# Layer 2 of a two-layer block kernel: attention by pairs of heads, with the products of two heads in turns in the two halves of the TensorE array

## The chip, the core and the metric

The kernel runs on one core of a Trainium2 chip. A core has a matrix engine (TensorE; PE in the profile), and VectorE (DVE), ScalarE (ACT), GpSimd (POOL) and SyncE (SP), each with an instruction queue of its own. Matmuls read SBUF and write PSUM; DMA queues bring the weights from device memory. The metric is the device time of one execution in microseconds; 0.2% of this kernel is 3.1 us.

## What is computed

The reference is two transformer blocks on a sequence of 256 tokens with a width of 1024. The first has a stick-breaking attention, a retention branch and a mixture of 32 experts; the change does not touch it. The second, cut to what matters:

```
h = rms_norm(x, norm1_pre)
q, k, v, z, xbc, dt_raw, gates = split(h @ w_in)      # 8 query heads and 2 key heads of 64; z, xbc: state space branch
attn_out = softmax(q k^T / 8) v                       # per head: 256 x 256 scores; then @ w_attn_proj
xs, bm, cm = split(silu(conv(xbc)))                   # 16 heads of 64, 2 groups, state 128
y = ssd_forward + ssd_backward + d_skip * xs          # per head: (C B^T * decay) X, and a term from the state
ssd_y = rms_norm(y * silu(z))                         # then @ w_ssd_proj
x += rms_norm((g_attn * attn_out + g_ssd * ssd_out) @ w_out)
x += rms_norm((silu(gate) * up) @ w_down)             # feed forward, width 2816
```

Two head loops matter here. Attention: for each of 8 heads the scores (256 x 256, from q and k of depth 64), a softmax, and the product with v (64 columns). State space: for each of 16 heads a 256 x 256 block-wise decay matrix, and its product with that head's 64 columns of `xs`.

## The kernel before

`mixer2` (layer 2 up to the first residual) runs two kinds of work woven into each other. The backbone is a row of large projections (`lin_t`, lines 241 to 243, tiles `pt_lin`; `lin`, lines 214 to 216): each weight chunk is brought by DMA into a ring (`raw`), split by ACT and DVE into a high and a low part (`whi`, line 168, and `wlo`, line 169, a ring of three), and multiplied in three matmuls. Between these steps stand small pieces: `decay`, `values`, `scores`, `probs`, `attend`, convolutions, norms. Table `STEPS2` gives each piece a place among the steps, `weave` calls it there, and a scheduler then fixes the order on every engine when the program is built, so what stands next to what on PE is not what the code's order alone says.

The pieces which the change touches:

- `decay(h)`, 16 heads: two matmuls make a log decay matrix `pr` (lines 1532 and 1533), ACT takes four exponentials into `E` (line 1538), DVE multiplies (line 1539), POOL adds the two directions (line 1541). Every second head adds a matmul `peb` (line 1546).
- `values(c)`, 8 pairs of heads: line 1560 multiplies `E` with 64 columns of `xs` into one half of the PSUM tile `py`: partitions 0 to 63 for the even head, 64 to 127 for the odd one. First both products of the even head, then both of the odd one. Line 1562 adds the state's product with the whole array. DVE then makes `y`.
- `scores(h)`, 8 heads: line 1577, two matmuls with a depth of 64 (the even head's q and k are in partitions 0 to 63, the odd head's in 64 to 127) into a PSUM tile `psc`; DVE takes the row maximum `mx` (lines 1579, 1580); ACT takes two exponentials with their sums (line 1585), DVE the reciprocal, ACT scales (line 1588): `prob`.
- `probs(h)`: four transposes (line 1596, tile `ptp`) and a copy `pT` by ACT (line 1598).
- `attend(h)`: line 1608, two matmuls with 64 columns of v into one half of the PSUM tile `pov`; after the odd head ACT and DVE split the result for the projection.
- `attn(i)`, ten steps: `scores(i)`, `probs(i - 1)`, `attend(i - 2)`.

A matmul that uses only half of the array's rows is shown as `64*128` in the profile, one that uses half of its columns as `128*64`, and one that uses the whole as `128*128`. Every fp32 matmul other than a transpose leaves two records (passes): 16 score matmuls are 32 records. The projections' matmuls leave one. The PSUM pool `pm` (tag `m`) has four buffers, shared by `psc`, `ptp`, `pov`, `pr`, `peb` and some others; SBUF tag `E` has four, shared by `E`, `prob` and `pT`.

Of the kernel before, what the change touches and what calls it, by code (L numbers as in the profile page):

```python
# [10 lines left out]
F32 = mybir.dt.float32  # L11
F32R = mybir.dt.float32r
I32 = mybir.dt.int32
AF = mybir.ActivationFunctionType
ALU = mybir.AluOpType
AX = mybir.AxisListType
PSUM = bass.MemoryType.PSUM
P = 128
D = 1024
T = 256  # L20
# [29 lines left out]
def blk(b):  # L50
    return slice(b * P, b * P + P)
# [40 lines left out]
class Net:  # L92
# [1154 lines left out]
    def mixer2(self):  # L1247
        nc, a, tc, xt = self.nc, self.a, self.tc, self.xt
        with ExitStack() as es:
            p1 = self.pool(es, "m2a")  # L1250
            p2 = self.pool(es, "m2b", 2)
            pw = self.pool(es, "pslinD", 3, space=PSUM)
            py_ = self.pool(es, "psyD", 1, space=PSUM)
            pm = self.pool(es, "psmD", 4, space=PSUM)
            w = a["w_in_2"][0]
            ident, ones = self.ident, self.ones
            K = {}
# [8 lines left out]
            def after(name):  # L1266
                return tc.issue_after(K[name].ins)

            def exps():
                return after("silu")  # L1270
# [56 lines left out]
            xs = p1.tile([P, 2, D], F32, name="xs")  # L1327
# [52 lines left out]
            bias = p1.tile([P, 2, 2, 16], F32, name="bias")  # L1380
# [74 lines left out]
            qT = p1.tile([P, 4, T], F32, name="qT", tag="qT")  # L1455
            kT = p1.tile([P, 2, T], F32, name="kT")
            vt = p1.tile([P, 2, P], F32, name="vt")
            Q = {}
# [51 lines left out]
            E, EB, ST = {}, {}, {}  # L1510
# [16 lines left out]
            def decay(h):  # L1527

                gg = h // 8
                pr = pm.tile([P, 2, 2, P], F32, name="pr", tag="m")  # L1530
                o = pr.rearrange("p d b l -> p (d b l)")
                nc.tensor.matmul(o, K["identr"], K["neg"], start=True, stop=False)
                nc.tensor.matmul(o, K["idr"][:, h:h + 1].to_broadcast([64, P]), K["at"].rearrange("p c l -> p (c l)"), start=False, stop=True)  # L1533
                x = p2.tile([P, 2, 2, P], F32, name="E", tag="E", bufs=4)
                for d in range(2):
                    for j in range(2):
                        with exps():
                            K["exp"] = nc.scalar.activation(x[:, d, j], pr[:, 1 - d, j], AF.Exp, bias=bias[:, d, 1 - j, h:h + 1])
                nc.vector.tensor_tensor(x.rearrange("p d b l -> p (d b) l"), x.rearrange("p d b l -> p (d b) l"),
                                        cb[:, :, :, gg].rearrange("p d b l -> p (d b) l"), op=ALU.mult)  # L1540
                nc.gpsimd.tensor_tensor(x[:, 0], x[:, 0], x[:, 1], op=ALU.add)
                E[h] = x
                if h % 2 == 0:
                    c = h // 2
                    pe = pm.tile([P, T], F32, name="peb", tag="m")
                    nc.tensor.matmul(pe, K["sel"][:, h:h + 2].rearrange("p i e -> p (i e)"),
                                     K["at"][:, 1:3].rearrange("p c l -> p (c l)"), start=True, stop=True)
                    eb = p2.tile([P, T], F32, name="EB")
                    with exps():
                        nc.scalar.activation(eb, pe, AF.Exp)  # L1550
                    EB[c] = eb

            def values(c):
                gg = c // 4
                py = py_.tile([P, 2, T], F32, name="py", tag="y")
                for i in range(2):
                    h = 2 * c + i
                    x = E.pop(h)
                    for b in range(2):
                        nc.tensor.matmul(py[i * 64:i * 64 + 64, 0, blk(b)], xs[:, b, h * 64:h * 64 + 64], x[:, 0, 1 - b], start=True, stop=True)  # L1560
                for b in range(2):
                    nc.tensor.matmul(py[:, 1, blk(b)], ST[gg][:, 1 - b, blk(c % 4)], xbc[2][:, 2 + gg, blk(b)], start=True, stop=True)
                o = y[:, c]
                nc.vector.scalar_tensor_tensor(o, xbc[gg][:, c % 4], K["dsk"][:, c:c + 1], py[:, 0], ALU.mult, ALU.add)
                t = p2.tile([P, T], F32, name="yo", tag="t1", bufs=4)
                nc.vector.tensor_tensor(t, py[:, 1], EB.pop(c), op=ALU.mult)
                nc.vector.tensor_tensor(o, o, t, op=ALU.add)


            O = []  # L1570

            def scores(h):
                i, c, kv = h % 2, h // 2, h // 4
                hs = slice(i * 64, i * 64 + 64)
                ps = pm.tile([P, 2, T], F32, name="psc", tag="m")
                for b in range(2):
                    nc.tensor.matmul(ps[:, b], qT[hs, c, blk(b)], kT[hs, kv, :], start=True, stop=True)  # L1577
                mx = self.sm.tile([P, 2], F32, name="mx")
                nc.vector.tensor_reduce(mx, ps, AX.X, ALU.max)
                nc.vector.tensor_scalar(mx, mx, -0.125, None, ALU.mult)  # L1580
                pr = p2.tile([P, 2, T], F32, name="prob", tag="E", bufs=4)
                sm = self.sm.tile([P, 2], F32, name="smm")
                for b in range(2):
                    with exps():
                        K["exp"] = nc.scalar.activation(pr[:, b], ps[:, b], AF.Exp, bias=mx[:, b:b + 1], scale=0.125, accum_out=sm[:, b:b + 1])
                nc.vector.reciprocal(sm, sm)
                for b in range(2):
                    nc.scalar.activation(pr[:, b], pr[:, b], AF.Copy, scale=sm[:, b:b + 1])
                Q["p", h] = pr

            def probs(h):
                pr = Q.pop(("p", h))
                pt = pm.tile([P, 2, T], F32, name="ptp2", tag="m")
                for sb in range(2):
                    for b in range(2):
                        nc.tensor.transpose(pt[:, sb, blk(b)], pr[:, b, blk(sb)], ident)
                pT = p2.tile([P, 2, T], F32, name="pT", tag="E", bufs=4)
                nc.scalar.copy(pT, pt)
                Q["pT", h] = pT

            def attend(h):
                i, c, kv = h % 2, h // 2, h // 4
                if i == 0:
                    Q["po"] = pm.tile([P, T], F32, name="pov", tag="m")
                po = Q["po"]
                pT = Q.pop(("pT", h))
                for sb in range(2):
                    nc.tensor.matmul(po[i * 64:i * 64 + 64, :], vt[:, sb, kv * 64:kv * 64 + 64], pT[:, sb], start=sb == 0, stop=sb == 1)  # L1608
                if i == 1:
                    if c == 0:  # L1610
                        O.extend(p1.tile([P, 4, T], F32R, name=f"o{j}", tag=f"cu{j}") for j in range(2))
                    self.hilo(O[0][:, c], O[1][:, c], po)

            def attn(i):
                for f, h in ((scores, i), (probs, i - 1), (attend, i - 2)):
                    if 0 <= h < 8:
                        f(h)


            z = p1.tile([P, 8, T], F32, name="z")  # L1620
# [49 lines left out]
            m = xs.rearrange("p b (c t) -> p (b c) t", t=T)  # L1670
# [20 lines left out]
            def gain():  # L1691
# [8 lines left out]
            at = lambda n, f, *args: (n, lambda: f(*args))  # L1700
            S = STEPS2
            row = lambda n, i: S[n][0] + S[n][1] * i
            pieces = [at(S["rows"], scale_rows), at(S["constants"], constants), at(S["rope"], rope_tables),
                      at(S["chain1"], chain1), at(S["chain2"], chain2), at(S["chain3"], chain3)]
# [6 lines left out]
            for h in range(16):  # L1711
                pieces.append(at(row("decay", h), decay, h))
                if h % 2 == 1:
                    pieces.append(at(row("values", h), values, h // 2))
            pieces += [at(S["states1"], states, 1), at(S["states1"] + 0.1, states2, 1)]
            pieces += [at(row("attn", i), attn, i) for i in range(10)]
            pieces += [at(row("sigmoid0", i), sigmoid, i) for i in range(4)]
            pieces += [p for c in range(9) for p in ([at(row("gate", c), gate_y, c)] if c < 8 else []) + ([at(row("gate", c), sum_y, c - 1)] if c else [])]
            pieces += [at(row("sigmoid1", i - 4), sigmoid, i) for i in range(4, 8)] + [at(46, gain)]
# [116 lines left out]
```

## Time and profile before

| | us |
|---|---|
| median of 3 runs (lowest to highest) | 1566.34 (1564.61 to 1567.75) |
| the profiled execution, its own time | 1566.19 |
| its span in the profile | 1564.3 |
| PE busy in the span | 1468.7 (94%) |
| DVE, ACT, POOL busy | 657.8, 457.2, 105.0 |
| stretch of layer 2's mixer in which the touched pieces run | about 1186 to 1294 |

The page gives busy time by engine, slices, DMA, a chain and the costliest groups. A timeline gives the records of one engine in order: start, time from the first start to the last end of the merged records, engine, line, operation, tile out<-in, shapes, count, and the idle time ahead with what ended it. PE's matmuls are pipelined: a record lasts longer than the distance to the next start, so distances between starts tell what the engine needs.

### The profile page before, as it was taken

How to read it: one execution, taken by the hardware profiler on the slowest of the kernel's cores; microseconds unless marked ns; L12 is line 12 of the kernel's file. 1: busy time of each engine (PE TensorE's matmuls, PEld its weight loads, DVE VectorE, ACT ScalarE, POOL GpSimd, SP SyncE). 2: the span in 40 equal slices, each digit the busy share in tenths (PEclk: the TensorE clock that was granted, in tenths of full speed). 3: DMA queues.
4: the chain of work that ended last, by engine and by line, in shares of the span. 5: the costliest groups of instructions: out<-in, count | busy, mean ns of one | idle time of the engine just before them, and what ended most of it. 6: DMA issues, size and time to landing. Idle time of an engine off the chain costs nothing. (4 is left out here: it accounts for less than half of the span.)

```text
span 1564.3 us, 19166 instructions
## 1 busy us (share of the span) xinstructions
PE 1468.7 (94%) x7695; PEld 851.2 (54%) x7695; DVE 657.8 (42%) x1200; ACT 457.2 (29%) x851; POOL 105.0 (7%) x217
## 2 busy tenths in 40 slices
PE   8999999999988988988899988888999999999998
PEld 6777434333333333333333333323888779899986
DVE  6666222232222222322221321223789567676654
ACT  7655110110100000100110100002676665564443
POOL 3220000000000000000000000000307100000000
PEclk9999999999999999999999999999999999999999
DMA  7826999999999999999999999997553324656551
GB/s 253 322 108 265 368 427 425 425 428 426 425 427 424 428 425 427 425 425 422 419 426 428 425 427 427 428 426 304 175 174 116 102 72 161 202 172 188 183 199 41
DMA packets 94288, 499.49 MB, mean 319 GB/s; under 512 B 10068, under 2 KB 34004, under 8 KB 67956
## 3 DMA queue, kind: packets, MB, share of 16 engines
q1 hardware_dynamic: 93763, 497.44, 79.5%
q8 instruction: 62, 1.02, 0.3%
q10 hardware_dynamic: 432, 0.79, 0.1%
q14 instruction: 31, 0.25, 0.0%
HBM read 497.15 MB, written 1.05 MB: 318 GB/s over the span
## 5 line engine op out<-in xcount | busy, mean ns | idle before, releaser
L853 PE MATMUL pu<-raw,xst 128*64 128x512 f32 x2048 | 456.1, 599 | 23.8 <-DMA raw<-in_w_up_gate_dram 23.7
L853 PEld LDWEIGHTS pu<-raw,xst 128*64 128x64 f32 x2048 | 143.6, 138 | 316.4 <-issue 273.4
L169 DVE TENSOR_TENSOR wlo<-raw,whi 128x1024 fp32r<-128x1024 f32 (+2 forms) x178 | 215.2, 1212 | 124.1 <-ACT whi L168 123.0
L890 PE MATMUL py<-raw,hT 128*64 128x512 f32 x1024 | 231.1, 598 | 35.8 <-DMA raw<-in_w_down_dram 34.4
L168 ACT CAST whi<-raw 128x1024 fp32r<-128x1024 f32 (+2 forms) x178 | 180.7, 1022 | 172.1 <-PE pt_lin L242 88.0
L859 DVE COPY u<-pu 128x512 f32<-128x512 f32 x32 | 22.1, 692 | 408.6 <-PE pu L853 408.6
L242 PE MATMUL pt_lin<-xl,whi 128*128 128x256 f32 x640 | 180.7, 284 | 0.0
L243 PE MATMUL pt_lin<-xh,wlo 128*128 128x256 f32 x640 | 178.9, 283 | 0.5 <-DVE wlo L169 0.5
L241 PE MATMUL pt_lin<-xh,whi 128*128 128x256 f32 x640 | 179.3, 285 | 0.0
L890 PEld LDWEIGHTS py<-raw,hT 128*64 128x64 f32 x1024 | 76.7, 138 | 185.3 <-issue 154.4
L872 DVE TENSOR_TENSOR h<-ph,bT 128x512 f32<-128x512 f32 x64 | 44.1, 689 | 245.5 <-PE ph L869 244.6
L858 ACT COPY u<-pu 128x512 f32<-128x512 f32 x32 | 18.7, 585 | 389.7 <-PE pu L853 389.7
L243 PEld LDWEIGHTS pt_lin<-xh,wlo 128*128 128x128 f32 x640 | 120.2, 189 | 4.2 <-issue 3.3
L242 PEld LDWEIGHTS pt_lin<-xl,whi 128*128 128x128 f32 x640 | 120.9, 189 | 2.6 <-issue 2.6
L241 PEld LDWEIGHTS pt_lin<-xh,whi 128*128 128x128 f32 x640 | 120.0, 189 | 3.8 <-issue 3.3
L896 ACT COPY yy<-py 64x512 f32<-64x512 f32 x32 | 18.5, 578 | 266.9 <-PE py L890 266.9
L904 PE MATMUL po<-yy,cg 128*128 128x512 f32 x128 | 62.8, 614 | 9.7 <-DVE xt L906 9.0
L876 ACT ACTIVATE sg<-h 128x256 f32<-128x256 f32 x64 | 26.7, 417 | 121.8 <-DVE h L874 121.8
L794 POOL TENSOR_TENSOR SG<-S,gates 128x256 f32<-128x256 f32 x16 | 10.9, 697 | 705.1 <-DVE h L874 655.7
L215 PE MATMUL ps_lin<-wlo,xh 128*128 128x512 f32 (+1 forms) x144 | 56.6, 396 | 0.0
L214 PE MATMUL ps_lin<-whi,xh 128*128 128x512 f32 (+1 forms) x144 | 53.9, 396 | 0.4 <-ACT vt L1469 0.4
L802 PE MATMUL pg<-S,hn 128*128 128x256 f32 x224 | 54.0, 385 | 0.2 <-ACT cg L831 0.2
(460 smaller groups left out, 1760.3 us busy)
## 6 DMA issues: line engine op xcount, KB each, us to landing
raw<-in_w_up_gate_dram SPq DMA_DIRECT2D x120, 2048.0 KB, 34.0
raw<-in_w_down_dram SPq DMA_DIRECT2D x59, 2048.0 KB, 32.7
raw<-in_w_in_dram SPq DMA_DIRECT2D x33, 1024.0 KB, 5.2
raw<-in_w_gate_up_dram SPq DMA_DIRECT2D x44, 512.0 KB, 4.1
raw<-in_w_down_dram SPq DMA_DIRECT2D x20, 1024.0 KB, 5.1
raw<-in_w_up_gate_dram SPq DMA_DIRECT2D x16, 1024.0 KB, 33.1
raw<-in_w_out_dram SPq DMA_DIRECT2D x8, 1024.0 KB, 5.1
raw<-in_w_ple_gate_dram SPq DMA_DIRECT2D x4, 1024.0 KB, 24.6
```

The lines of the kernel that those rows point to most:

```text
L168: a = self.nc.scalar.copy(hi, src)
L169: b = self.nc.vector.tensor_tensor(lo, src, f32(hi), op=ALU.subtract)
L214: nc.tensor.matmul(ps[b][:, :n], xh[:, k, xs], hi[:, c, :n], start=k == 0, stop=False)
L215: nc.tensor.matmul(ps[b][:, :n], xh[:, k, xs], lo[:, c, :n], start=False, stop=False)
L241: nc.tensor.matmul(o, hi[:, c, cs], xh[:, k, :], start=k == 0 and j % 2 == 0, stop=False, skip_group_check=True)
L242: nc.tensor.matmul(o, hi[:, c, cs], xl[:, k, :], start=False, stop=False, skip_group_check=True)
L243: nc.tensor.matmul(o, lo[:, c, cs], xh[:, k, :], start=False, stop=k == nk - 1, skip_group_check=True)
L802: nc.tensor.matmul(flat(ps[:, kk]), hn[:, b, blk(2 * k2 + kk)], flat(S[g][b]), start=b == 0 and kk == 0, stop=b == 1, skip_group_check=True)
L853: nc.tensor.matmul(ps[j][q * 64:q * 64 + 64], xst[:, k, i], raw[:, half(2 * q + j)], start=k == 0, stop=k == 7, skip_group_check=True)
L872: nc.vector.tensor_tensor(h, ph, bT[:, :, o:o + 3:2].unsqueeze(3).to_broadcast([P, 4, 2, SLOTS]), op=ALU.add)
L890: i = nc.tensor.matmul(py[n * 64:n * 64 + 64], hT[:, k], raw[k % 4][:, half(n)], start=k == 0, stop=k == 7, skip_group_check=True)
L904: nc.tensor.matmul(po, CG[c][:, blk(b)], Y[c][:, n], start=True, stop=True)
```

## The change

`scores`, and `attend` with it, take a pair of heads instead of one. `scores(c)` takes two `psc` tiles and issues, for each block, the even head's matmul and then the odd one's; the softmax of both heads follows. `attend(c)` issues, for each block of keys, the odd head's product and then the even one's, into the two halves of one `pov`. `values(c)` issues its four products in turns likewise. `attn` has twelve steps in place of ten: a pair of scores in each even step up to 6, `probs(i - 2)`, and `attend` of a pair in odd steps from 5. Tag `E` gets seven buffers in place of four, and the small tiles `mx` and `smm` get four in place of two. The numbers in `STEPS2` stay, and the number of matmuls on every line stays.

```diff
             def values(c):
                 gg = c // 4
                 py = py_.tile([P, 2, T], F32, name="py", tag="y")
-                for i in range(2):
-                    h = 2 * c + i
-                    x = E.pop(h)
-                    for b in range(2):
-                        nc.tensor.matmul(py[i * 64:i * 64 + 64, 0, blk(b)], xs[:, b, h * 64:h * 64 + 64], x[:, 0, 1 - b], start=True, stop=True)
+                x = [E.pop(2 * c + i) for i in range(2)]
+                for b in range(2):
+                    for i in (1, 0):
+                        h = 2 * c + i
+                        nc.tensor.matmul(py[i * 64:i * 64 + 64, 0, blk(b)], xs[:, b, h * 64:h * 64 + 64], x[i][:, 0, 1 - b], start=True, stop=True)
...
-            def scores(h):
-                i, c, kv = h % 2, h // 2, h // 4
-                hs = slice(i * 64, i * 64 + 64)
-                ps = pm.tile([P, 2, T], F32, name="psc", tag="m")
+            def scores(c):
+                kv = c // 2
+                ps = [pm.tile([P, 2, T], F32, name="psc", tag="m") for _ in range(2)]
                 for b in range(2):
-                    nc.tensor.matmul(ps[:, b], qT[hs, c, blk(b)], kT[hs, kv, :], start=True, stop=True)
-                mx = self.sm.tile([P, 2], F32, name="mx")
-                nc.vector.tensor_reduce(mx, ps, AX.X, ALU.max)
...
+                    for i in range(2):
+                        hs = slice(i * 64, i * 64 + 64)
+                        nc.tensor.matmul(ps[i][:, b], qT[hs, c, blk(b)], kT[hs, kv, :], start=True, stop=True)
+                for i in range(2):
+                    mx = self.sm.tile([P, 2], F32, name="mx", bufs=4)
+                    nc.vector.tensor_reduce(mx, ps[i], AX.X, ALU.max)
...
+                    pr = p2.tile([P, 2, T], F32, name="prob", tag="E", bufs=7)
...
-            def attend(h):
...
+            def attend(c):
+                kv = c // 2
+                po = pm.tile([P, T], F32, name="pov", tag="m")
+                pT = [Q.pop(("pT", 2 * c + i)) for i in range(2)]
                 for sb in range(2):
-                    nc.tensor.matmul(po[i * 64:i * 64 + 64, :], vt[:, sb, kv * 64:kv * 64 + 64], pT[:, sb], start=sb == 0, stop=sb == 1)
-                if i == 1:
...
+                    for i in (1, 0):
+                        nc.tensor.matmul(po[i * 64:i * 64 + 64, :], vt[:, sb, kv * 64:kv * 64 + 64], pT[i][:, sb], start=sb == 0, stop=sb == 1)
...
             def attn(i):
-                for f, h in ((scores, i), (probs, i - 1), (attend, i - 2)):
-                    if 0 <= h < 8:
-                        f(h)
+                if i % 2 == 0 and i < 8:
+                    scores(i // 2)
+                if 0 <= i - 2 < 8:
+                    probs(i - 2)
+                if i % 2 == 1 and 0 <= i // 2 - 2 < 4:
+                    attend(i // 2 - 2)
...
-            pieces += [at(row("attn", i), attn, i) for i in range(10)]
+            pieces += [at(row("attn", i), attn, i) for i in range(12)]
```

On PE, the third pair's scores and the products before them stand like this in the order of before (numbers behind a name count its buffers; `pt_lin` are the projections' matmuls):

```order
L1577 MATMUL psc<-kT,qT 128x256 x2
L243 MATMUL pt_lin<-xh,wlo 128x256
L241 MATMUL pt_lin<-xh,whi 128x256
L242 MATMUL pt_lin<-xl,whi 128x256
L243 MATMUL pt_lin<-xh,wlo 128x256
L241 MATMUL pt_lin<-xh,whi 128x256
L242 MATMUL pt_lin<-xl,whi 128x256
L1596 MATMUL ptp_7445<-ident,prob 128x128 x4
L1608 MATMUL pov<-pT,vt 64x256 x2
L243 MATMUL pt_lin<-xh,wlo 128x256
```

and the third pair in the order of after:

```order
L243 MATMUL pt_lin<-xh,wlo 128x256
L1579 MATMUL psc<-kT,qT 128x256 x4
L241 MATMUL pt_lin<-xh,whi 128x256
L242 MATMUL pt_lin<-xl,whi 128x256
L243 MATMUL pt_lin<-xh,wlo 128x256
L1599 MATMUL ptp_7442<-ident,prob 128x128 x4
```

Two visits to the score product, of one head each and with the rest of the order between them, have become one visit of both heads. Later on, the product with v likewise stands as one row of four:

```order
L1610 MATMUL pov<-pT,vt 64x256 x4
L1532 MATMUL pr<-neg,identr 128x512
L1533 MATMUL pr<-at,idr 128x512
L242 MATMUL pt_lin<-xl,whi 128x256
```

In the second pair the scheduler has put three projection matmuls between the two heads, on PE in the order of after:

```order
L1579 MATMUL psc<-kT,qT 128x256 x2
L243 MATMUL pt_lin<-xh,wlo 128x256
L241 MATMUL pt_lin<-xh,whi 128x256
L242 MATMUL pt_lin<-xl,whi 128x256
L1579 MATMUL psc<-kT,qT 128x256 x2
```

The first `values` stands on PE in the order of before behind the transposes `pxs` for the even head, and apart from it for the odd one:

```order
L1355 MATMUL pxs<-ident,xbc_6003 128x128 x4
L1560 MATMUL py<-E,xs 64x128 x2
L242 MATMUL pt_lin<-xl,whi 128x256
L243 MATMUL pt_lin<-xh,wlo 128x256
L241 MATMUL pt_lin<-xh,whi 128x256
L242 MATMUL pt_lin<-xl,whi 128x256
L243 MATMUL pt_lin<-xh,wlo 128x256
L1532 MATMUL pr<-neg,identr 128x512
```

In the order of after the row of the even head is gone from there, and projection matmuls have moved up in front of the odd head's first product, in all four more of them:

```order
L1355 MATMUL pxs<-ident,xbc_6003 128x128 x4
L242 MATMUL pt_lin<-xl,whi 128x256
L243 MATMUL pt_lin<-xh,wlo 128x256
L241 MATMUL pt_lin<-xh,whi 128x256
L242 MATMUL pt_lin<-xl,whi 128x256
L243 MATMUL pt_lin<-xh,wlo 128x256
L241 MATMUL pt_lin<-xh,whi 128x256
L242 MATMUL pt_lin<-xl,whi 128x256
L243 MATMUL pt_lin<-xh,wlo 128x256
L241 MATMUL pt_lin<-xh,whi 128x256
L1532 MATMUL pr<-neg,identr 128x512
```

On ACT, the first pair's softmax stands in the order of before in two parts, with the weight split `whi` between them:

```order
L1585 ACTIVATE prob,smm<-psc,mx 128x256 x2
L1538 ACTIVATE E<-pr,bias 128x128 x8
L1588 ACTIVATE prob<-prob,smm 128x256 x2
L168 CAST whi<-raw 128x1024
L1585 ACTIVATE prob,smm<-psc,mx 128x256 x2
L1550 ACTIVATE EB<-peb 128x256
```

and in the order of after in one:

```order
L1588 ACTIVATE prob,smm<-psc,mx 128x256 x4
L1538 ACTIVATE E<-pr,bias 128x128 x8
L1591 ACTIVATE prob<-prob,smm 128x256 x2
L168 CAST whi<-raw 128x1024
L1591 ACTIVATE prob<-prob,smm 128x256 x2
```

Two more exponentials now stand ahead of that split. From the first layer up to the first `values`, and from the last head's product with v to the end, the order on PE is that of before.

## Rows read from the trace of the kernel before

**Rows 1.** Stretches: length, busy us of PE, PEld, DVE, ACT, POOL; then PE clock.

```profile
1180.00:1200.00 20.00, 19.51 (x131) 16.09 (x129) 17.15 (x27) 15.96 (x34) 16.50 (x18) 1.00 0.33 106
1200.00:1290.00 90.00, 89.96 (x571) 69.34 (x572) 57.31 (x100) 56.42 (x143) 14.77 (x16) 1.00 0.28 88
1290.00:1340.00 50.00, 50.00 (x422) 49.54 (x421) 36.36 (x53) 27.31 (x43) 0.71 (x1) 1.00 0.50 169
```

**Rows 2.** Timeline of PE, then of POOL, around the first `values`.

```profile
1200.04 0.43 PE L1560 MATMUL py<-E,xs 128*64 128x128 f32 x2 [0.53 <-POOL E L1541]
...
1194.70 4.60 POOL L1485 TENSOR_TENSOR s<-q,rs_q 128x128 f32<-128x128 f32 x4
1199.26 0.73 POOL L1541 TENSOR_TENSOR E<-E 128x256 f32<-128x256 f32 x1
```

**Rows 3.** Timeline of ACT: scaling of a head's probabilities, and the next split.

```profile
1217.19 0.97 ACT L1588 ACTIVATE prob<-prob,smm 128x256 f32<-128x256 f32 x2
1219.12 1.05 ACT L168 CAST whi<-raw 128x1024 fp32r<-128x1024 f32 x1 [0.96 <-PE pt_lin L242]
```

**Rows 4.** Score passes by tile: ns min/median/max, first and last start.

```profile
L1577 PE MATMUL psc<-kT,qT x32: 375/376/481, 1210.8 to 1272.9; 64*128 64x256 f32 x32
```

**Rows 5.** PE's timeline: scores behind another half-array matmul; then between projections.

```profile
1212.35 0.59 PE L1577 MATMUL psc<-kT,qT 64*128 64x256 f32 x2
...
1262.71 0.28 PE L243 MATMUL pt_lin<-xh,wlo 128*128 128x256 f32 x1
1262.83 0.28 PE L241 MATMUL pt_lin<-xh,whi 128*128 128x256 f32 x1
1263.04 1.13 PE L1577 MATMUL psc<-kT,qT 64*128 64x256 f32 x4
1264.09 0.38 PE L242 MATMUL pt_lin<-xl,whi 128*128 128x256 f32 x1
1264.32 0.28 PE L243 MATMUL pt_lin<-xh,wlo 128*128 128x256 f32 x1
```

**Rows 6.** Timeline of PE: one head's product with v between projections.

```profile
1289.50 0.28 PE L243 MATMUL pt_lin<-xh,wlo 128*128 128x256 f32 x1
1289.71 1.08 PE L1608 MATMUL pov<-pT,vt 128*64 128x256 f32 x4
1290.71 0.39 PE L241 MATMUL pt_lin<-xh,whi 128*128 128x256 f32 x1
1290.94 0.28 PE L242 MATMUL pt_lin<-xl,whi 128*128 128x256 f32 x1
```

**Rows 7.** Timeline of PE: `values` and product with v in turns, different halves.

```profile
1253.93 0.32 PE L1560 MATMUL py<-E,xs 128*64 128x128 f32 x1
1253.94 0.43 PE L1608 MATMUL pov<-pT,vt 128*64 128x256 f32 x1
1254.09 0.38 PE L1560 MATMUL py<-E,xs 128*64 128x128 f32 x2
...
1254.31 0.27 PE L1560 MATMUL py<-E,xs 128*64 128x128 f32 x1
```

**Rows 8.** Timeline of PE, layer 1's scores: one head (77.27), two (56.02).

```profile
77.27 0.70 PE L589 MATMUL z<-qk 64*128 64x256 f32 x2
...
56.02 0.71 PE L589 MATMUL z<-qk 64*128 64x256 f32 x4
```

**Rows 9.** Timeline of PE, layer 1's values: one head (81.75), two (125.55).

```profile
81.75 0.65 PE L596 MATMUL py<-wt,dv 128*64 128x256 f32 x2
...
125.55 0.66 PE L596 MATMUL py<-wt,dv 128*64 128x256 f32 x4
```

**Rows 10.** Timeline of PE: `values` of one head (1258.33), two (1208.19).

```profile
1258.33 0.65 PE L1560 MATMUL py<-E,xs 128*64 128x128 f32 x4
...
1208.19 0.67 PE L1560 MATMUL py<-E,xs 128*64 128x128 f32 x8
```

**Rows 11.** PE's timeline: transposes of the probabilities of rows 3.

```profile
1221.63 0.27 PE L1596 MATMUL ptp<-ident,prob 128*128 128x128 f32 x1
```

More of the change, by code (lines that the diff above doesn't have):

```diff
@@ L1533, in decay @@
                 nc.tensor.matmul(o, K["idr"][:, h:h + 1].to_broadcast([64, P]), K["at"].rearrange("p c l -> p (c l)"), start=False, stop=True)
-                x = p2.tile([P, 2, 2, P], F32, name="E", tag="E", bufs=4)
+                x = p2.tile([P, 2, 2, P], F32, name="E", tag="E", bufs=7)
                 for d in range(2):
@@ L1570, in mixer2 @@
             O = []
-            def scores(h):
-                i, c, kv = h % 2, h // 2, h // 4
-                hs = slice(i * 64, i * 64 + 64)
-                ps = pm.tile([P, 2, T], F32, name="psc", tag="m")
+            def scores(c):
+                kv = c // 2
+                ps = [pm.tile([P, 2, T], F32, name="psc", tag="m") for _ in range(2)]
                 for b in range(2):
-                    nc.tensor.matmul(ps[:, b], qT[hs, c, blk(b)], kT[hs, kv, :], start=True, stop=True)
-                mx = self.sm.tile([P, 2], F32, name="mx")
-                nc.vector.tensor_reduce(mx, ps, AX.X, ALU.max)
[L1580 to L1589, printed above, removed]
+                    for i in range(2):
[4 more added lines that the diff above has]
+                    nc.vector.tensor_reduce(mx, ps[i], AX.X, ALU.max)
+                    nc.vector.tensor_scalar(mx, mx, -0.125, None, ALU.mult)
+                    pr = p2.tile([P, 2, T], F32, name="prob", tag="E", bufs=7)
+                    sm = self.sm.tile([P, 2], F32, name="smm", bufs=4)
+                    for b in range(2):
+                        with exps():
+                            K["exp"] = nc.scalar.activation(pr[:, b], ps[i][:, b], AF.Exp, bias=mx[:, b:b + 1], scale=0.125, accum_out=sm[:, b:b + 1])
+                    nc.vector.reciprocal(sm, sm)
+                    for b in range(2):
+                        nc.scalar.activation(pr[:, b], pr[:, b], AF.Copy, scale=sm[:, b:b + 1])
+                    Q["p", 2 * c + i] = pr
             def probs(h):
@@ L1596, in probs @@
                         nc.tensor.transpose(pt[:, sb, blk(b)], pr[:, b, blk(sb)], ident)
-                pT = p2.tile([P, 2, T], F32, name="pT", tag="E", bufs=4)
+                pT = p2.tile([P, 2, T], F32, name="pT", tag="E", bufs=7)
                 nc.scalar.copy(pT, pt)
                 Q["pT", h] = pT
-            def attend(h):
[L1602 to L1606, printed above, removed]
-                for sb in range(2):
-                    nc.tensor.matmul(po[i * 64:i * 64 + 64, :], vt[:, sb, kv * 64:kv * 64 + 64], pT[:, sb], start=sb == 0, stop=sb == 1)
-                if i == 1:
-                    if c == 0:
-                        O.extend(p1.tile([P, 4, T], F32R, name=f"o{j}", tag=f"cu{j}") for j in range(2))
-                    self.hilo(O[0][:, c], O[1][:, c], po)
-            def attn(i):
-                for f, h in ((scores, i), (probs, i - 1), (attend, i - 2)):
-                    if 0 <= h < 8:
-                        f(h)
+            def attend(c):
+                kv = c // 2
+                po = pm.tile([P, T], F32, name="pov", tag="m")
+                pT = [Q.pop(("pT", 2 * c + i)) for i in range(2)]
+                for sb in range(2):
+                    for i in (1, 0):
+                        nc.tensor.matmul(po[i * 64:i * 64 + 64, :], vt[:, sb, kv * 64:kv * 64 + 64], pT[i][:, sb], start=sb == 0, stop=sb == 1)
+                if c == 0:
+                    O.extend(p1.tile([P, 4, T], F32R, name=f"o{j}", tag=f"cu{j}") for j in range(2))
+                self.hilo(O[0][:, c], O[1][:, c], po)
+            def attn(i):
+                if i % 2 == 0 and i < 8:
[4 more added lines that the diff above has]
+                    attend(i // 2 - 2)
             z = p1.tile([P, 8, T], F32, name="z")
```

## The prediction, made before the changed kernel was run

> **What bounds the kernel now.** I read the busy times by stretch first, since a mean over the whole span mixes very different stages. The touched pieces run between about 1186 and 1294 us. There PE is busy 19.51 of 20 us, then 89.96 of 90, then all of 50, at the full granted clock, while DVE and ACT are busy some 60% of the time and POOL hardly at all after 1200 [rows 1]. A busy PE is not yet a PE at its peak, so the next view is its timeline: the records follow each other at the distance that the passes need, and the only idle time noted on it from 1186 to 1300 is 0.53 us at the first `values` [rows 2]. The other engines wait for PE rather than PE for them: the weight split on ACT at 1219.12 had stood for 0.96 us until PE gave back a buffer [rows 3]. So PE is what ends last. What its queue loses here, the kernel loses, and everything behind moves up, unless a wait takes the place of the work.
>
> **What one visit to half the array costs.** A score pass lasts 0.376 us [rows 4] and two in a row, where the array already stood in halves, take 0.59 [rows 5]: the second starts 0.215 us behind the first, and that is what a pass of 256 columns needs. From the last projection start ahead of a head's scores to the second one behind them is 1264.32 - 1262.83 = 1.49 us [rows 5]. Two projection steps are in it, 0.12 us each (1262.71 to 1262.83), and four passes, 0.86. The remaining 0.39 us is the way to the half array and back. For the product with v the same sum is 1.44 - 0.24 - 0.86 = 0.34 us [rows 6]. So a change of tile shape costs 0.17 to 0.20 us; I take 0.18. A pass of 128 columns needs 0.11 us (two take 0.38, one lasts 0.27 [rows 7]).
>
> **Do two heads share the time of one?** The trace of before already holds this. Halves of the rows: in layer 1 the scores of one head (two passes) last 0.70 us, those of two heads side by side (four passes) 0.71 [rows 8]. Halves of the columns: two passes 0.65 us, four 0.66 [rows 9]. And on line 1560 itself: four passes of one head 0.65 us, eight of two heads 0.67 [rows 10]. A shared pass therefore costs about 0.01 us instead of its own 0.215 or 0.11. In the last pair one head's matmuls were all issued ahead of the other's: turns in the code are not needed for sharing, neighbours in the order are.
>
> The Trainium skill has a rule against half of this: "TensorE: Matmul & The Clock Gate", in Part 3 on packing small matmuls, says that weight loads overlap with running matmuls only where the row group differs. Column halves have the same row group, so by it `values` and `attend` would gain nothing from sharing. [Rows 9, 10] show the opposite, and the rule's case is weighed among the rivals.
>
> **The change, term by term.**
>
> 1. Scores: 32 passes. Before, no two heads are neighbours, all 32 stand alone. In the order of after three of the four pairs are together (one in two pieces, both heads in each); the second pair has three projection matmuls between its heads. So 12 passes are shared: 12 x (0.215 - 0.01) = 2.5 us off.
> 2. Product with v: 32 passes. In the order of after three pairs are together and half of the last one (a small row-sum product stands in it): 14 shared passes, 14 x 0.205 = 2.9 us off.
> 3. `values`: 64 passes. After, 30 are shared (all pairs but half of the first). Before, 8 already were (two full pairs), and 6 more stood beside products with v in the other half, which hid them too [rows 7]. 30 - 14 = 16 passes newly shared, 16 x 0.10 = 1.6 us off. The term is small because the scheduler had found part of it already.
> 4. Changes of tile shape, counted in the two orders from the first `pst` to the last `pss`: 95 before, 78 after. 17 x 0.18 = 3.1 us off; by the bounds 2.9 to 3.4.
> 5. A wait that grows. The first odd head's `E` leaves POOL at 1199.99, and PE waits 0.53 us for it [rows 2]. POOL's order is the same after, and what it does there (the rotation of q, 4.60 us ahead of that `E`) begins before PE has come to anything that changed, so this moment stands. PE comes to it earlier: the even head's four passes with their two changes (0.44 + 0.34) are no longer ahead of it, four more projection steps (0.47) are. That is 0.31 us more of waiting: 0.3 us on. Behind PE there stand the transposes of k, so these wait too; their time is in the same sum.
> 6. Softmax on ACT and DVE: the same instructions, two heads at a time. The first pair puts four exponentials instead of two ahead of the next weight split. That split was waiting for PE [rows 3], and with three buffers a split that waits for PE has two units of 24 projection matmuls ahead, 2 x 24 x 0.12 = 5.8 us of PE's work; two exponentials more, and a maximum, are 1 to 2 us. The transposes start 3.5 us after their probabilities are ready (1217.19 + 0.97 to 1221.63, [rows 3, 11]). Both covers hold by these rows, so I set it near nothing (0.3 us), with up to 4 us, 1 us for each pair, if they don't. A gain here is excluded, since PE waited for none of it.
> 7. Tag `E` with seven buffers, small tiles with four: no instructions, so nothing on PE. SP's and POOL's orders stay as they were. If the 90 us of [rows 1] become 80, ACT's 56 us and DVE's 57 us are 71% of them, so neither becomes the bound.
>
> Sum: 2.5 + 2.9 + 1.6 + 3.1 - 0.3 - 0.3 = 9.5 us. From the last head's product with v on, PE's order is that of before, so the rest moves as a block. The profiled execution's 1566.19 becomes 1556.7. It stands 0.15 us under the median of the three runs, so the same number serves for the median.
>
> **Rivals.**
>
> - *The covers are too thin (lost leads).* Two score tiles at once take two of the four PSUM buffers of `pm`, and both heads' maxima and exponentials must end before `pr` or `ptp` gets them. The second pair, which the scheduler has torn apart, speaks for it; the leads of [rows 3, 11] against it. With 1 us for each of four pairs and 1 more for the torn one, 9.8 - 5 = 4.8 gives 1561.4.
> - *Column halves don't share here.* Items 2 and 3 fall, 9.5 - 4.5 = 5.0 us, 1561.2. [Rows 9, 10] speak against it on matmuls of the same shape. This is the case of the skill's rule above.
> - *The change doesn't do what it says:* neither half shares in the new order, and only the changes of shape are saved: 3.1 - 0.3 gives 1563.4. Turns could do this if the hardware wanted one head's passes in a block; [rows 7], where two products stand in turns and share, speak against it.
> - *Slower: ACT's queue starves the projections.* A pair's four exponentials wait for the second head's maximum, with eight exponentials of `E` and the next `whi` queued behind them. If each of some nine splits in the stretch came later than the 5.8 us of work that PE has ahead, PE would stand at each. To end above 1569.3 the waits must eat the 9.8 us and 3.1 more, 1.4 us at each split beyond that cover; such a case ends at about 1570. ACT at 63% busy [rows 1] speaks against it.
>
> **How the numbers follow.** The forecast (9.5 us, between 8 and 10.5 by the bounds of items 4 and 6 and a us of scatter between runs) gets 0.76; lost leads 0.13; no sharing in the columns 0.03; no sharing at all 0.04; slower 0.04. The forecast's own span is 1555 to 1559. The range reaches to the lost leads: 1554.7 to 1561.4. 0.2% of this kernel is 3.1 us, about what a measurement can tell from no change. Faster by more than that is below 1563.2: forecast, lost leads and the columns' case, 0.92, of which I take 0.04 off for causes that I haven't named; 0.88. Within 0.2% is 0.08, slower 0.04.
>
> **What would show it.** In the timeline of after, eight score passes in one row of about 1.1 us where four took 1.13; eight products with v in about 1.1; every `values` but the first with eight passes in 0.67. The wait for POOL at the first `values` should be about 0.8 us and nearly all of PE's idle time up to the last `pss`; the last `pss` group should come about 9.5 us earlier, and all behind it by the same. If the rows of pairs last 2 us, sharing was wrong; if they are short and PE shows waits for ACT or DVE, the covers were.

## The result, and the profile after

The changed kernel takes 1550.42 us (median of six runs, 1546.97 to 1552.52); the kernel before took 1566.31 beside it. The ratio is 0.9897, 95% interval 0.9882 to 0.9912. That is 15.9 us less where 9.5 were forecast: the sign was right, but the time lies below the range. The profiled execution took 1551.04 us, its span is 1549.2. One slow run of `e9_ring_down` (next section), of 6556 us, stands in no ratio.

The head of the page of the changed kernel, with the busy time of each engine, and then two stretches of the lengths of [rows 1], each begun 3.5 us earlier, as the work ahead of the change ends earlier (length, busy us of PE, PEld, DVE, ACT, POOL; PE clock, DMA share, GB/s):

```profile
span 1549.2 us, 19157 instructions
PE 1452.8 (94%) x7695; PEld 843.2 (54%) x7695; DVE 656.0 (42%) x1200; ACT 456.0 (29%) x851; POOL 106.6 (7%) x217
```

```profile
1196.50:1286.50 90.00, 90.00 (x657) 73.62 (x658) 64.03 (x114) 63.11 (x159) 14.79 (x16) 1.00 0.35 112
1286.50:1336.50 50.00, 50.00 (x402) 48.89 (x401) 36.13 (x48) 24.28 (x33) 0.71 (x1) 1.00 0.52 169
```

PE is still full at the full clock, and the 90 us now hold 657 matmuls where [rows 1] had 571; DVE and ACT fill 71% and 70% of them, about as item 7 had worked out. PE waits once between the first `pst` and the last `pss`; this is the whole answer of its waits in that window (total, times, longest):

```profile
PE py L1560 <- POOL E L1541: 0.9, 1, 0.9
```

The rows of the pairs, in PE's timeline of the changed kernel (start, time, engine, line, tile, form, count):

```profile
1235.28 0.28 PE L243 MATMUL pt_lin<-xh,wlo 128*128 128x256 f32 x1
1235.49 1.14 PE L1579 MATMUL psc<-kT,qT 64*128 64x256 f32 x8
1236.56 0.39 PE L241 MATMUL pt_lin<-xh,whi 128*128 128x256 f32 x1
1236.78 0.28 PE L242 MATMUL pt_lin<-xl,whi 128*128 128x256 f32 x1
...
1261.11 0.28 PE L243 MATMUL pt_lin<-xh,wlo 128*128 128x256 f32 x1
1261.31 1.08 PE L1610 MATMUL pov<-pT,vt 128*64 128x256 f32 x8
1262.33 0.38 PE L241 MATMUL pt_lin<-xh,whi 128*128 128x256 f32 x1
1262.55 0.28 PE L242 MATMUL pt_lin<-xl,whi 128*128 128x256 f32 x1
...
1204.39 0.66 PE L1560 MATMUL py<-E,xs 128*64 128x128 f32 x8
```

Eight score passes take 1.14 us where four took 1.13 [rows 5]; from the last projection start ahead to the second behind it is 1236.78 - 1235.28 = 1.50 us, before 1.49. Eight products with v take 1.08, four took 1.08 [rows 6], and the same distance is 1.44 in both. A second head costs nothing that these rows can show. The second pair, torn by three projections, pays for two visits:

```profile
1218.65 1.13 PE L1579 MATMUL psc<-kT,qT 64*128 64x256 f32 x4
1219.70 0.39 PE L243 MATMUL pt_lin<-xh,wlo 128*128 128x256 f32 x1
1219.93 0.28 PE L241 MATMUL pt_lin<-xh,whi 128*128 128x256 f32 x1
1220.05 0.28 PE L242 MATMUL pt_lin<-xl,whi 128*128 128x256 f32 x1
1220.26 1.13 PE L1579 MATMUL psc<-kT,qT 64*128 64x256 f32 x4
```

**Where the time went.** The first `pst` and the last group of `pss` enclose all touched work. In PE's timeline they stand, in before, in the changed kernel, and in two kernels of the next section (`e2_unshifted`, `e1_small4`), at:

```profile
1185.04 0.59 PE L1524 MATMUL pst<-xw,bt 128*128 128x512 f32 x1
...
1316.79 0.50 PE L1658 MATMUL pss<-ones,y 128*128 128x1 f32 x4
```

```profile
1181.50 0.59 PE L1524 MATMUL pst<-xw,bt 128*128 128x512 f32 x1
...
1302.70 0.50 PE L1662 MATMUL pss<-ones,y 128*128 128x1 f32 x4
```

```profile
1185.37 0.59 PE L1524 MATMUL pst<-xw,bt 128*128 128x512 f32 x1
...
1306.88 0.50 PE L1662 MATMUL pss<-ones,y 128*128 128x1 f32 x4
```

```profile
1180.28 0.59 PE L1524 MATMUL pst<-xw,bt 128*128 128x512 f32 x1
...
1311.55 0.50 PE L1658 MATMUL pss<-ones,y 128*128 128x1 f32 x4
```

The stretch took 131.75 us before and takes 121.20 now: 10.55 us of the 15.1 by which the two spans differ, 1 us more than forecast. But 3.54 us are there already at the first `pst`, ahead of any touched work, and 1.0 more come behind the last `pss`, where PE's order did not change. These 4.5 us are most of what the prediction missed. Of the 3.54 us, 2.78 stand already at layer 2's first projection (in before, then in the changed kernel), so they come from layer 1 and the experts:

```profile
1116.04 0.48 PE L241 MATMUL pt_lin<-xh,whi 128*128 128x256 f32 x2
```

```profile
1113.26 0.48 PE L241 MATMUL pt_lin<-xh,whi 128*128 128x256 f32 x2
```

### The profile page after: what moved, and what is told of

Its sections match the earlier page's. It is cut to its first block, busy times and chain, and to the rows that moved or that the text cites. A ratio compares the mean times of both kernels' runs of the same rounds, so it can differ in the third digit from the quotient of the medians.

```text
span 1549.2 us, 19157 instructions
## 1 busy us (share of the span) xinstructions
PE 1452.8 (94%) x7695; PEld 843.2 (54%) x7695; DVE 656.0 (42%) x1200; ACT 456.0 (29%) x851; POOL 106.6 (7%) x217
```

## The experiments

Each ran beside the kernel before on the same chip; its median there was 1564.6 to 1564.9 us. Ratios are to it, with their 95% intervals. "The stretch" is first `pst` to last `pss` as above.

### Where do the 4.5 us outside the stretch come from?

The changed kernel has four buffers instead of two for `mx` and `smm`. They lie in a pool at the start of SBUF (each buffer takes 32 bytes of a partition), so the weight ring and nearly all large tiles lie 128 bytes higher. `e1_small4` is the kernel before with this alone, and the same order on every engine:

```
-                mx = self.sm.tile([P, 2], F32, name="mx")
+                mx = self.sm.tile([P, 2], F32, name="mx", bufs=4)
...
-                sm = self.sm.tile([P, 2], F32, name="smm")
+                sm = self.sm.tile([P, 2], F32, name="smm", bufs=4)
```

> The kernel before, with four buffers in place of two for the small tiles mx and smm and nothing else. The order on every engine is that of before; all larger SBUF tiles, the weight ring raw among them, lie 128 bytes higher, as they do in the changed kernel. The traces of before and after differ by 15.1 us, of which 3.57 us are there already at the first pst, ahead of any changed work. Theory 'placement': these come from where the tiles lie, so this kernel is about 4 us faster than before (1562). Theory 'scatter': they are chance between runs, so it is within 1 us of 1566.3.

1559.2 us, 0.9962 (0.9949 to 0.9975): 5.4 us faster without any change of an instruction's order. `e2_unshifted` is the reverse: the changed kernel with `smm` in layer 2's own pool, so that the first pool, with `mx` at four buffers, is as large as before and the large tiles lie where they lay:

```
-                    sm = self.sm.tile([P, 2], F32, name="smm", bufs=4)
+                    sm = p2.tile([P, 2], F32, name="smm", tag="smm2", bufs=4)
```

> The changed kernel with the four buffers of smm taken from another pool, so that the weight ring lies where it lay before; the order on every engine is that of the changed kernel. Theory 'placement': some 4 us slower than the changed kernel, about 1555, and the first pst starts at the time of before. Theory 'scatter': as the changed kernel, 1550 give or take 1.5.

1556.13 us, 0.9942 (0.9929 to 0.9955). Its first `pst` is at 1185.37 (before: 1185.04) and its stretch 121.51 us, 10.24 shorter than before; `e1_small4`'s is 0.48 shorter. So the pairs bring the stretch's 10 us in that trace (8.5 us by the medians, 7.0 to 11.1 by the interval), and the place of the tiles brings what the changed kernel has beyond it. Placement holds, scatter falls.

### The parts of the change

`e3_values_only` is before with the new `values` alone, `e4_attn_only` the changed kernel with the old `values`, each by a swap of these lines (in `e4_attn_only` the other way round):

```
-                for i in range(2):
-                    h = 2 * c + i
-                    x = E.pop(h)
-                    for b in range(2):
...
+                x = [E.pop(2 * c + i) for i in range(2)]
+                for b in range(2):
+                    for i in (1, 0):
```

> The kernel before with the turns in values alone; attention by single heads. By the prediction's prices: 28 shared slots of values where before had 12, 88 changes of tile shape where before had 95: 16 x 0.10 less 6 slots that stood beside products with v and now do not, + 7 x 0.18 = 2.3 us, about 1564. If the column halves did not share: 1.3 us, 1565. If the saving above the prediction's 9.5 us sits in values: 1561 or less.

> The changed kernel with values as before (both products of one head, then both of the other), attention by pairs. The scheduler then keeps 16 slots of values shared, 8 of scores and 12 of the product with v, with 86 changes of tile shape: 6.0 us in the stretch by the prediction's prices, about 1560. Buffers as in the changed kernel, so with 'placement' 4 us more: 1556.

`e3_values_only`: 1562.75 us, 0.9988 (0.9980 to 0.9997); its stretch is 2.6 us shorter where 2.3 were expected. `e4_attn_only`: 1554.4 us, 0.9931 (0.9915 to 0.9948); 7.1 us shorter in the stretch where 6.0 were expected, and with the tiles 128 bytes higher: 34% of the projection steps there are short ones (see below), against 3% in before, which by estimate, at 5 ns a step, is 0.9 us. The terms follow the orders.

`e8_block` asks whether turns are needed. In all three pieces the loop over heads goes outside:

```
-                for b in range(2):
-                    for i in (1, 0):
+                for i in (1, 0):
+                    for b in range(2):
...
```

> The changed kernel with the turns taken out: in scores, attend and values all matmuls of one head are issued ahead of all of the other, still as neighbours. The scheduler keeps as many shared slots (30 of values, 12 of scores, 16 of the product with v, two more) and has 76 changes of tile shape where the changed kernel has 78. If neighbours are enough for sharing, as the prediction says: as the changed kernel, up to 0.8 us faster in the stretch. If turns are needed: some 6 us slower in the stretch (7.0 us of sharing by items 1 to 3, less what before had).

1551.26 us, 0.9902 (0.9886 to 0.9918): no different from the changed kernel. Its stretch is 0.6 us shorter than that of the changed kernel, for two more shared passes and two changes of shape less. Neighbours share; turns are not needed here.

### What is it about the place?

First the distance. `e5_down128` takes `mx` and `smm` from layer 2's pool (all 128 bytes lower), `e6_up64` and `e7_up96` give `mx` four and five buffers:

```
-                mx = self.sm.tile([P, 2], F32, name="mx")
+                mx = p2.tile([P, 2], F32, name="mx", tag="mx2", bufs=2)
...
-                sm = self.sm.tile([P, 2], F32, name="smm")
+                sm = p2.tile([P, 2], F32, name="smm", tag="smm2", bufs=2)
```

```
-                mx = self.sm.tile([P, 2], F32, name="mx")
+                mx = self.sm.tile([P, 2], F32, name="mx", bufs=5)
```

> The kernel before with mx and smm taken from the pool of layer 2, so that the weight ring and the other large tiles lie 128 bytes lower than before; the order on every engine is that of before. With 128 bytes more (e1_small4) the kernel was 5.4 us faster. Theory 'position within 256 bytes': 128 down is the same position as 128 up, so about 5 us faster than before (1559). Theory 'higher is better' or 'the end of the space': no gain, 1564.6 or slower.

> The kernel before with four buffers for mx alone: tiles 64 bytes higher, the same order. Position theory in steps of 64 bytes: some gain of its own, between 0 and 5.4 us; if 128 bytes are the step (position only 0 or 128 within 256): as before, 1564.6.

> The kernel before with five buffers for mx: tiles 96 bytes higher, so that the weight ring begins at a multiple of 128 bytes (18304) where it lay 32 above one (18208); the same order. If alignment to 128 bytes is what counts: faster than with 128 bytes up, by more than 5.4 us. If the gain grows with the distance: 4 us. If only the position within 256 counts in steps of 128: 0.

128 bytes down gain no less than 128 up do (9.0 and 5.4 us, with intervals that overlap), 64 up nothing, 96 up a little, 2.7 us, which is none of the sizes that were expected for it (table below). So it is not the distance, and alignment to 128 is not it either.

Then the tiles. `e9_ring_down` puts a gap behind layer 2's weight ring into `e5_down128`, so that there only the ring is moved. `e12_operands_up` puts the same gap into the kernel before, so that the ring and everything before layer 2 stay, and `xh`, `xl` and what lies behind them move. `e13_gap_behind` puts it behind `xh` and `xl`, in both halves of layer 2. `e14_gap256`, `e15_gap224` and `e16_gap192` are `e12_operands_up` with wider gaps.

```
         net.ring, net.halves, net.pair = net.pool(ctx, "ringb", 5), 1, []
+        net.pool(ctx, "gap", 1).tile([P, 32], F32, name="gap")
```

```
             xl = p1.tile([P, 8, T], F32R, name="xl", tag="xl")
+            p1.tile([P, 32], F32, name="gap")
```

> As e5_down128 (9.0 us faster than before), but with a gap of 128 bytes behind the weight ring of layer 2, so that there only the ring lies 128 bytes lower, while xh, xl, hh, hl and all else of layer 2 lie where they lie in the kernel before. Layer 1 and the experts are as in e5_down128. In e5_down128 the projections' matmuls start 113 ns apart in 1116:1182 and 1360:1470 where before had 118, and the stretch from the last pss to the last down projection's first matmul is 3.7 us shorter. Theory 'operands' (the place of the stationary xh and xl counts): back to 118 ns, that stretch back to 178.8 us, about 5 us of the 9.0 gone, 1560.5. Theory 'ring' (the place of the transfers' target counts): 113 ns stay, 1556.

> The kernel before with a gap of 128 bytes behind the weight ring of layer 2 and nothing else: there xh, xl and all tiles behind them lie 128 bytes higher, the ring and all of layer 1 and of the experts where they lay. Theory 'operands': the projections in 1116:1182 step at 113 ns as in e1_small4, and 2 to 2.5 us of its 5.4 remain, 1562.5. Theory 'ring': 118 ns, 1564.9.

> As e12_operands_up (5.3 us faster than before), but the gap of 128 bytes stands behind xh and xl in both halves of layer 2: xh and xl, which the projections' matmuls read as the moving operand, lie where they lie in before, all tiles behind them 128 bytes higher. Theory 'moving operand': the projections step at 118 ns again and the kernel is as before, 1564.8. Theory 'other tiles' (softmax, decay, split results): as e12_operands_up, 1559.5.

> The kernel before with a gap of 256 bytes behind the weight ring of layer 2: xh and xl start 32 bytes behind a multiple of 256, as in before, all else of layer 2 lies 256 bytes higher. Theory 'position within 256 bytes': no gain, 118 ns a step, 1564.8. Theory 'any move helps': as e12_operands_up, 1559.5.

> The kernel before with a gap of 224 bytes: xh and xl start at a multiple of 256 bytes. Theory 'alignment': the fastest place, 113 ns in most steps, 5 us or more. Theory 'only 160 within 256': 118 to 119 ns and 0 to 2 us, as e6_up64 and e7_up96 (96 and 128 within 256) have shown.

> The kernel before with a gap of 192 bytes: xh and xl start 224 bytes behind a multiple of 256. If the distance to the position of before (32) counts: between before and e12_operands_up, some 2 us. If odd multiples of 32 behind a half of 256 (160 to 224) are good: 5 us.

All of them have PE's order of before. The second column is where `xh` and `xl` of layer 2, the moving operands of the projections' matmuls, start within 256 bytes, by the program's allocation. The last shows in how many of the pairs of neighbouring projection matmuls the second starts at most 115 ns after the first, in the profiled execution: from the experts' end to the first `pst` (310 pairs), in the stretch (558), and from there to the last down projection (1277). The stationary operands `whi` and `wlo` have the same addresses in all these kernels.

| kernel | `xh`, `xl` | us | ratio | short steps |
|---|---|---|---|---|
| before | 32 | 1564.6 to 1564.9 | 1 | 9%, 3%, 2% |
| e14_gap256 | 32 | 1564.91 | 0.9997 (0.9987 to 1.0006) | 9%, 3%, 2% |
| e13_gap_behind | 32, tiles behind them moved | 1563.09 | 0.9991 (0.9981 to 1.0000) | 4%, 1%, 2% |
| e9_ring_down | 32, ring and layer 1 moved | 1563.23 | 0.9990 (0.9980 to 0.9999) | 9%, 3%, 2% |
| e6_up64 | 96 | 1564.81 | 1.0001 (0.9993 to 1.0010) | 12%, 14%, 17% |
| e7_up96 | 128 | 1562.19 | 0.9982 (0.9974 to 0.9991) | 9%, 12%, 18% |
| e16_gap192 | 224 | 1566.55 | 1.0009 (0.9999 to 1.0019) | 1%, 2%, 2% |
| e15_gap224 | 0 | 1563.96 | 0.9989 (0.9979 to 0.9999) | 12%, 12%, 27% |
| e12_operands_up | 160 | 1559.49 | 0.9967 (0.9956 to 0.9978) | 48%, 31%, 2% |
| e1_small4 | 160 | 1559.20 | 0.9962 (0.9949 to 0.9975) | 83%, 32%, 7% |
| e5_down128 | 160 | 1555.93 | 0.9947 (0.9935 to 0.9960) | 88%, 32%, 82% |

The three kernels at 160 are the three that gain clearly. Moving layer 2's operands with what lies behind them is enough (`e12_operands_up`: 5.3 us, twice what was expected of it); leaving them and moving what lies behind, or the ring, is not; moving them by 256 bytes is not. The operands by themselves were not moved. `e9_ring_down` steps at 118 ns again and keeps 1.6 of the 9.0 us, less than the 4 that were expected to stay. The theory "moving operand" holds against "ring", "other tiles" and "any move helps". In `e15_gap224` alignment to 256 was expected to be best by one theory, and is not; `e16_gap192`, at 224, was expected to gain 2 or 5 us and gains nothing. The trace of `e12_operands_up` is of its slowest run (1563.77 us), so it does not show where all of the 5.3 us lies.

One sees it in PE's timeline as the distance of starts, first in before and then in `e5_down128`, at the same place of the last projections:

```profile
1400.05 0.28 PE L241 MATMUL pt_lin<-xh,whi 128*128 128x256 f32 x1
1400.17 0.28 PE L242 MATMUL pt_lin<-xl,whi 128*128 128x256 f32 x1
1400.29 0.28 PE L243 MATMUL pt_lin<-xh,wlo 128*128 128x256 f32 x1
1400.40 0.28 PE L241 MATMUL pt_lin<-xh,whi 128*128 128x256 f32 x1
```

```profile
1400.27 0.28 PE L241 MATMUL pt_lin<-xh,whi 128*128 128x256 f32 x1
1400.38 0.28 PE L242 MATMUL pt_lin<-xl,whi 128*128 128x256 f32 x1
1400.49 0.28 PE L243 MATMUL pt_lin<-xh,wlo 128*128 128x256 f32 x1
1400.60 0.28 PE L241 MATMUL pt_lin<-xh,whi 128*128 128x256 f32 x1
```

Three steps take 0.35 us there and 0.33 here, 118 and 113 ns each by the records' medians. Windows count the same: PE's busy time, matmuls, granted clock, DMA share and GB/s, of before, of the changed kernel and of `e5_down128`:

```profile
1137.00:1152.00 15.00, 15.00 (x130) 1.00 0.46 150
...
1380.00:1460.00 80.00, 80.00 (x681) 1.00 0.62 196
```

```profile
1134.00:1149.00 15.00, 15.00 (x135) 1.00 0.46 152
1380.00:1460.00 80.00, 80.00 (x681) 1.00 0.61 186
```

```profile
1380.00:1460.00 80.00, 80.00 (x709) 1.00 0.63 193
```

PE is 100% busy at the full clock in all five rows, and yet does 4% more matmuls in two of them. The place does not settle it alone: at 160 whole blocks of projections step at 113 or at 118 ns (`e5_down128` has 82% short steps in its last part, `e1_small4` 7%), and at 32 the stretch of `e2_unshifted` has 17% short steps, that of before 3%.

The place of tiles acts in an earlier stage too, without layer 2's `xh` and `xl`. The experts' down products (line 890), first and last start, in before and in `e12_operands_up`, where the tiles of layer 1 and the experts lie as before, and then in the changed kernel and in `e9_ring_down`, where they are moved:

```profile
L890 PE MATMUL py<-raw,hT x1024: 592/592/1116, 199.3 to 1080.4; 128*64 128x512 f32 x171
```

```profile
L890 PE MATMUL py<-raw,hT x1024: 592/592/1061, 199.4 to 1079.6; 128*64 128x512 f32 x171
```

```profile
L890 PE MATMUL py<-raw,hT x1024: 592/592/1116, 198.2 to 1077.6; 128*64 128x512 f32 x171
```

```profile
L890 PE MATMUL py<-raw,hT x1024: 592/592/1061, 198.2 to 1076.5; 128*64 128x512 f32 x171
```

They take 881.1, 880.2, 879.4 and 878.3 us. Over all profiled executions it is 879.9 to 881.0 us in the eight kernels with these tiles unmoved, and 878.0 to 879.6 in the ten with them moved. Which tile does it is not shown.

### Do the two gains add up?

`e10_after_down` is the changed kernel, and `e11_block_down` is `e8_block`, with `mx` and `smm` from layer 2's pool as in `e5_down128`.

> The changed kernel with mx and smm taken from the pool of layer 2, as in e5_down128: the large tiles lie 128 bytes lower than before, 256 lower than in the changed kernel; the order on every engine is that of the changed kernel. If pairing and placement add up: 8.5 us (e2_unshifted) and 9.0 us (e5_down128), 1564.9 - 17.5 = 1547.4, some 3 us faster than the changed kernel. If they don't: 1550 to 1551.

> e8_block (no turns, 76 changes of tile shape) with the tiles 128 bytes lower than before, as in e5_down128. As e10_after_down, up to 0.8 us less in the stretch: 1546.6 to 1547.4; the fastest if the terms add up.

`e10_after_down`: 1551.48 us, 0.9914 (0.9899 to 0.9930). The 17.5 us expected were added wrongly: the changed kernel's `xh` and `xl` lie at 160 already, 128 higher, and 256 bytes lower they lie at 160 again. By position the two are the same kernel, and their intervals overlap. `e11_block_down`: 1546.35 us, the lowest median of all, but 0.9896 (0.9882 to 0.9911) is the changed kernel's ratio; its profiled execution had the short step in the last projections (83%), that of `e10_after_down` had not (7%). That it beats the changed kernel is not shown.

## Why the prediction was right or wrong

**What bounds the kernel: right.** PE's only wait in the stretch is the one for POOL, before and after.

**Items 1 to 3, sharing: right.** The visits of eight passes are as long as those of four. The rule of the Trainium skill that the prediction weighed ("TensorE: Matmul & The Clock Gate", Part 3) says that weight loads overlap with running matmuls only where the row group differs; that `values` and `attend`, whose heads have the same row group, would then gain nothing was the prediction's reading of it. Eight products with v in 1.08 us speak against that reading, as [rows 9, 10] had. Both rivals that doubt sharing fall with these rows.

**Item 4, tile shapes: held in the sum.** No run measures a change of shape alone.

**The size: a little low.** The stretch should have become 9.5 us shorter; with the tiles where they were it became 10.24 shorter in one trace (`e2_unshifted`). 0.3 us of the rest is item 6, priced at 0.3 and worth nothing. The remaining 0.4 is, by estimate, what the short steps make: they are 17% of the steps in that kernel's stretch, 3% in before's, and 14% of 556 steps at 5 ns are 0.4 us.

**Item 5, the wait for POOL: right.** Forecast 0.84 us, measured:

```profile
1196.47 0.43 PE L1560 MATMUL py<-E,xs 128*64 128x128 f32 x2 [0.86 <-POOL E L1541]
```

**Item 6, the covers: they held.** Neither a lost lead nor a starved queue shows up. On ACT, a pair's second pair of exponentials follows on the first, eight of `E` come next, and no matmul waits for the split `whi` behind them:

```profile
1212.64 0.47 ACT L1588 ACTIVATE prob<-psc,mx 128x256 f32<-128x256 f32 x1
1213.00 0.20 ACT L1588 ACTIVATION_READ_ACCUMULATOR prob<-psc,mx 128x1 f32 x1
1213.09 0.48 ACT L1588 ACTIVATE prob<-psc,mx 128x256 f32<-128x256 f32 x1
1213.45 0.21 ACT L1588 ACTIVATION_READ_ACCUMULATOR prob<-psc,mx 128x1 f32 x1
1213.54 2.19 ACT L1538 ACTIVATE E<-pr,bias 128x128 f32<-128x128 f32 x8
1215.54 0.98 ACT L1591 ACTIVATE prob<-prob,smm 128x256 f32<-128x256 f32 x2
1216.34 1.11 ACT L168 CAST whi<-raw 128x1024 fp32r<-128x1024 f32 x1
```

**Item 7, the buffers: this is the step that failed.** "No instructions, so nothing on PE": it is true that no instruction and no order came from them, but four more small buffers moved nearly every large tile by 128 bytes, and this is worth 5.4 us (`e1_small4`). By the medians the place of layer 2's `xh` and `xl` and the tiles behind them can make as much (`e12_operands_up`, 5.3 us); in the changed kernel's trace, where the last projections step at 118 ns, more than half of the 4.5 us lies ahead of layer 2's first projection. Without the move the 9.5 us forecast stand against the 8.5 of `e2_unshifted`; that its 1556.13 us lies so near the 1556.7 forecast is in part luck, since the kernel before took 1564.62 beside it and not the 1566.19 from which the forecast was taken. The step that "the rest moves as a block" fell with item 7: the order was the same, the pace was not. The range was drawn from waits that could be lost and held no cause outside the touched stretch; 1 us of scatter was all that stood for one.

**Still open.** Why a block of projections steps at 113 or 118 ns at one and the same place is not settled, nor is what the place of the tiles does in the experts' stage. How the gain divides between the two is not shown either: layer 2's tiles from `xh` on gain 5.3 us (`e12_operands_up`), the ring and the tiles of the earlier stages 1.6 (`e9_ring_down`), both together 5.4 or 9.0 (`e1_small4`, `e5_down128`), each with an interval of some 2 us to either side. Single traces also carry chance. In before the granted clock is at 0.50, the lower level of 1.2 GHz, for 3.4 us at the first projections, behind a wait of PE of 1.90 us for ACT. `e14_gap256`, at the same place, has 1.00 throughout and is 1.6 us shorter from its first projection to the first `pst`:

```profile
1116.40:1119.80 3.40, 3.40 (x19) 0.50 0.17 28
1116.04:1185.04 69.00, 67.08 (x494) 0.98 0.57 184
```

```profile
1115.43:1182.87 67.44, 65.51 (x494) 1.00 0.58 188
```

In the changed kernel's trace the clock falls at the same point (0.50 from 1114.3 on), so this does not part it from before. The seven buffers of `E` were not tried apart.

## What to carry to other kernels

Products that fill half the array cost next to nothing here beside their counterpart in the other half, if the final order makes them neighbours; whether their matmuls stood in turns made no difference. A change of a buffer count or a tile's size can move everything allocated behind it: compare the addresses too, and before crediting a gain to the edit, run the old kernel with the new layout alone. Start with stretches that the edit doesn't touch: a difference there is the sign.

## What was not expected of the hardware

A projection matmul of 128x256 (one pass) starts 118 ns after the one before it when its moving operand starts 32 bytes behind a multiple of 256, and in many blocks 113 ns after it when it starts at 160; the granted clock is 1.00 and PE is busy 100% in both. Over the kernel that is 5 us of 1565, and positions 0, 96, 128 and 224 lie between 1.7 us slower and 2.7 us faster than 32. From the last `pss` to the first matmul of the last down projection it is 178.8 us in before's profile and 175.0 in that of `e5_down128`, although the granted clock is at 0.51 there for 3.4 us (from 1364.3 on). The runs also spread wider: five to seven runs of a kernel at 160 differ by 4.3 to 9.5 us in all eight such kernels, five to eleven runs of the others by 2.4 to 4.2.
